# Attention and convolution with fewer VectorE operations, and a chunk mask written into PSUM by VectorE

## The chip, the cores and the metric

The kernel runs on one core of a Trainium2 chip. The metric is the device time of one execution in microseconds. TensorE (PE) multiplies into PSUM; VectorE (DVE) and ScalarE (ACT) read PSUM and SBUF and prepare the next operands; GpSimd (POOL) clears a few buffers, and SyncE (SP) issues the weight loads. Each engine works through its own instructions in the order in which the program lists them, and waits for results of the others through semaphores.

## The reference

Two transformer-like blocks on 512 positions of width 1024, in fp32. The first has 16 meta tokens ahead of the sequence, so 528 positions. The parts that the change touches:

```python
# block 1, differential attention, 8 heads, two maps (m) of width 64 per head, query blocks of 128
s = jnp.einsum('bqhmd,bkhmd->bhmqk', qb * HEAD_DIM ** -0.5, kf)
mask = cid[None, :] <= qc[:, None]                # chunks of 64 positions: no later chunk is seen
p = jax.nn.softmax(jnp.where(mask, s, NEG_INF), axis=-1)
a = p[:, :, 0] - lam * p[:, :, 1]
o = jnp.einsum('bhqk,bkhe->bqhe', a, vf)          # then an RMS norm per head and a gate
# block 1, beside it: a causal depthwise convolution over 31 positions, 1024 channels, with bias
# block 2, third part of its mixer: attention of 4 heads of width 64 over keys chosen by top-k,
#   under the same chunk rule; its first query block sees all admissible keys
```

The convolution's result goes through a layer norm over the channels and a SiLU into the product with `w_conv_out`; that product, gated, is added to the attention's result, and the sum goes into `w_out`. A gated FFN with a short convolution follows. Block 2 has a mixer of three parts (a matrix memory, a linear recurrence and the attention above) and again an FFN.

## The kernel before

The activations lie transposed, channels on the 128 partitions and positions along the free dimension. A weight tile of 1024 x 128 is loaded by SyncE, split by ScalarE (`wh`) and VectorE (`wl`) into two parts, and multiplied in three products per 128 rows (`step`), so that a unit of 128 output channels is 48 products of some 256 columns (`units`, `one`). All products stand on line 314 of the profile, all transposes on line 320, and all VectorE and ScalarE work on line 158, where a wrapper (`Lane`) records it; so rows are told apart by tile names.

The order of the work is made by the Python program itself. It keeps an estimated time for TensorE (`self.pe`), VectorE and ScalarE and an estimated ready time for every tile (`Model`, with 0.13 us from the end of an operation to its use by the next). The main line issues the units; after each group of products `tick` resumes the background tasks, generators that yield the time until their operands are due (`due`). VectorE's background list `bg` is emptied one operation at a time whenever VectorE's estimated time is at most 0.3 us ahead of TensorE's. `until` lets TensorE's estimated time run on until a condition holds. What is fixed so is the order on each engine; on the chip the engines wait for each other where an operand is late.

Block 1's mixer (`block1_mix`) runs 8 convolution units of two weight tiles (`glu`), 32 attention units (q, k, v and gate of 8 heads, `head`) and 8 gate units, in the order of `units1`: one convolution unit, three attention units, and so on, and six gate units at the end. After each convolution unit VectorE forms `u` from PSUM (`e_a`) and the 33 operations of `conv_ops` go into `bg`: a scaling with bias into `a`, a scaling into `b`, 29 taps that alternate between `a` and `b`, `a + b`, and the running sum `csum`. When `bg` is empty after the eighth, `after_conv` starts `layer_norm`: sums over channels, squares, and `finish`, three tasks that produce `us[0]` to `us[7]`. The units of `w_conv_out` (`pairs`) need `us[k]` one after the other; the first two units run together and finish with `us[7]`.

`attention` has two tasks for a head. `softmax(i)` computes the scores of query tile i for both maps (64 rows of the array each) in fp32, adds the mask by a bf16 product of `ind` (ones in one row) with `neg` (-1e30 in 64 columns) for the last 64 keys of the first 64 queries, takes the row maximum, scales it by -0.125 (`nb`) and runs the exponential on ScalarE, with the row sums in `l`. Tile 0 also multiplies the first two queries of the sequence (`sx`). Tiles 0 to 2 hold both maps in one PSUM buffer, tile 3 one map at a time. The second task weighs the two maps (`weigh`), transposes, multiplies by the values, and scales by the norm's factor `sc` in one VectorE operation. Block 2's attention (`sparse`) does the same per head and query tile with three tasks at once; tile 0 is masked by `ind` and `neg`, the others by an identity product with a mask tile. Each step takes a fresh buffer `eT`.

Of the kernel before, what the change touches and what calls it, by code (L numbers as in the profile page):

```python
# [17 lines left out]
P = 128  # L18
# [144 lines left out]
class Build:  # L163
# [159 lines left out]
    def constants(self):  # L323
        nc, c = self.nc, self.const
        self.ident = c.tile([P, P], F32, name="ident")
        make_identity(nc, self.ident)
        self.identb = c.tile([P, P], BF, name="identb")
        nc.vector.tensor_copy(self.identb, self.ident)
        self.ones = c.tile([P, P], F32, name="ones")
        nc.vector.memset(self.ones, 1.0)  # L330
        self.ind = c.tile([P, P], BF, name="ind")
        nc.vector.memset(self.ind, 0.0)
        for m in range(2):
            nc.vector.memset(self.ind[64 * m : 64 * m + 1, 0:64], 1.0)
        self.neg = c.tile([P, 64], BF, name="neg")
        nc.vector.memset(self.neg, NEG)
# [416 lines left out]
    def conv_ops(self, j, u, a, b, csum):  # L753
        V = self.V
        w = lambda k: self.col("conv_dw_w", k * 8 + j)
        ops = [
            lambda: V.tensor_scalar(a, u[:, 0:NQ], w(0), self.col("conv_dw_b", j), op0=MUL, op1=ADD),
            lambda: V.tensor_scalar(b, u[:, 1 : 1 + NQ], w(1), None, op0=MUL),
        ]
        for k in range(2, CK):  # L760
            d = a if k % 2 == 0 else b
            ops.append(lambda k=k, d=d: V.scalar_tensor_tensor(d, u[:, k : k + NQ], w(k), d, op0=MUL, op1=ADD))
        ops.append(lambda: V.tensor_tensor(a, a, b, op=ADD))
        if j == 0:
            ops.append(lambda: V.tensor_copy(csum, a))
        else:
            ops.append(lambda: V.tensor_tensor(csum, csum, a, op=ADD))
        return ops

    def attention(self, tp, h, qk, vs, ctx):  # L770
# [5 lines left out]
        made, used = [], [0]  # L776
        mask = lambda m: (self.ind[64 * m : 64 * m + 64, :], self.neg[64 * m : 64 * m + 64, :])
# [3 lines left out]
        def softmax(i):  # L781
            L = 144 + 128 * i
            q = lambda m: qT[64 * m : 64 * m + 64, 2 + 128 * i : 130 + 128 * i]
            mx, nb, l = self.sm(2, "mx"), self.sm(2, "nb"), self.sm(2, "ll")
            e = self.slot()

            def ex(m, sv):
                S.activation(e[:, m, :L], sv, AF.Exp, bias=nb[:, m : m + 1], scale=0.125, accum_out=l[:, m : m + 1])

            yield self.due(qT)  # L790
            if i < 3:
                i_at, pt = yield from self.at_get()
                for m in range(2):
                    mm(pt[:, 512 * m : 512 * m + L], q(m), k(m, 0, L), True, False)
                for m in range(2):
                    mm(pt[:, 512 * m + L - 64 : 512 * m + L], *mask(m), False, True)
# [12 lines left out]
                self.at_put(i_at)  # L809
            else:  # L810
                for m in range(2):
                    i_at, pt = yield from self.at_get()
                    mm(pt[:, 248:512], q(m), k(m, 0, 264), True, True)
                    mm(pt[:, 512:776], q(m), k(m, 264, 528), True, False)
                    mm(pt[:, 712:776], *mask(m), False, True)
                    yield self.due(pt)
                    V.tensor_reduce(mx[:, m : m + 1], pt[:, 248:776], axis=AX.X, op=MAX)
                    V.tensor_scalar(nb[:, m : m + 1], mx[:, m : m + 1], -0.125, None, op0=MUL)
                    yield self.due(nb)
                    ex(m, pt[:, 248:776])  # L820
                    self.at_put(i_at)
            return e, l
# [7 lines left out]
        def second():  # L830
# [11 lines left out]
            rl0, ss0 = self.sm(4, "rl0"), self.sm(4, "ss0")  # L842
# [46 lines left out]
            v = self.sm(4, "ssv")  # L889
# [6 lines left out]
            o3 = lambda q: o_sb[:, q, :512].rearrange("p (t e) -> p t e", e=P)  # L896
            V.tensor_tensor(o3(1), o3(0), sc[:, :, None].to_broadcast([P, 4, P]), op=MUL)
# [12 lines left out]
    def first_queries(self, ctx, xa, yav):  # L910
# [9 lines left out]
        S.activation(s3, s3, AF.Exp, scale=0.125)  # L920
# [119 lines left out]
    def block1_mix(self, raw):  # L1040
        nc, tc, io, V, S = self.nc, self.tc, self.io, self.V, self.S
        with ExitStack() as es:
# [41 lines left out]
            def glu(s):  # L1084
# [4 lines left out]
                def e_a(p):  # L1089
                    while len(self.bg) > CK + 2:  # L1090
                        self.bg.pop(0)()
# [6 lines left out]
                    self.bg.extend(self.conv_ops(s, u[:, Q0:], cvv(s), hold["tb"][:, 1, :NQ], csum))  # L1098
# [21 lines left out]
            def head(h, i):  # L1120
                def e_q(p):
# [3 lines left out]
                    S.activation(hold["qk"][:, 0, :NQ], p, AF.Copy)  # L1125
# [309 lines left out]
    def block2_mix(self):  # L1435
# [7 lines left out]
        with ExitStack() as es:  # L1443
# [275 lines left out]
            osb, todo = [], list(range(16))  # L1719

            def sparse(n):
# [17 lines left out]
                mx, nb, l, rl = (self.sm(1, x, bufs=5) for x in ("smx", "snb", "sll", "srl"))  # L1739
                V.tensor_reduce(mx, o, axis=AX.X, op=MAX)  # L1740
                V.tensor_scalar(nb, mx, -0.125, None, op0=MUL)
                yield self.due(nb)
                e = tp.tile([P, 3 + SEQ], F32, name=self.nm("e"), tag="lx", bufs=5)
                S.activation(e[:, :L], o, AF.Exp, bias=nb, scale=0.125, accum_out=l)
# [6 lines left out]
                eT = self.flat(SEQ)  # L1751
# [11 lines left out]
            def sparses():  # L1763
                yield from wait("av")
                if not osb:
                    osb.append(self.flat(1024).rearrange("p (t e) -> p t e", e=256))
# [26 lines left out]
            def done(name, o):  # L1793
# [9 lines left out]
                elif kind in ("iq", "mq", "aq", "ak", "lg"):  # L1803
# [6 lines left out]
                    tt(B[kind][-1], o, RB, MUL)  # L1810
# [391 lines left out]
```

## Time and profile before

| | |
|---|---|
| three runs, us | 1582.47, 1582.70, 1582.87 |
| the profiled execution, us | 1582.17 |
| its span, first to last instruction, us | 1580.4 |
| PE, PE weight loads, DVE, ACT, POOL busy, us | 1561.0, 1397.7, 1116.5, 650.8, 26.2 |
| granted TensorE clock, mean | 0.999 |

Busy times are unions of an engine's instructions; a line's "mean ns" is the duration of one instruction, and neighbours overlap, so what an instruction costs its engine is read from its start to the start of the next. In the timeline a merged line "x6" has the time from the first start to the last end. "Idle before" and the views of waits name what ended an engine's idle time. The stages of the span are: loading and first norm to 40 us, block 1's convolution and attention to 367, its layer norm and last attention head to 463, output products and FFN to 700 and on to about 1000, block 2's mixer to 1160, block 2's FFN to the end.

### The profile page before, as it was taken

To read this page: it belongs to the slowest core of one execution; us is meant where nothing else is said; L and a number is where in the kernel's file an instruction comes from. 1 tells how busy PE (TensorE), PEld (TensorE's weight loads), DVE (VectorE), ACT (ScalarE), POOL (GpSimd) and SP (SyncE) were. 2 spreads that over 40 slices of the span, in tenths; PEclk is the share of its full clock that TensorE was granted. 3 is DMA by queue.
4 is the path that set the end of the run, shared out by engine and by line. 5 is a ranking of instruction groups with operands and counts; after the bars stand their busy time and mean duration, and the time that the engine had idled before them with its cause. 6 is when DMAs were issued, how large, how long until landed. Compare 5 with 4: busy or idle time off the path is not lost.

```text
span 1580.4 us, 25476 instructions
## 1 busy us (share of the span) xinstructions
PE 1561.0 (99%) x10349; PEld 1397.7 (88%) x10349; DVE 1116.5 (71%) x2083; ACT 650.8 (41%) x1166; POOL 26.2 (2%) x89
## 2 busy tenths in 40 slices
PE   7999999999999999999999999999999999999998
PEld 6999999999999999999988877797799888888886
DVE  4989999997864676767743357898868877775224
ACT  5344434445542344434432222635466544444122
POOL 3000000000000000000000000000000000000000
PEclk9999999999999999999999999999999999999999
DMA  4322222222222323333333332231054133333221
GB/s 144 95 64 71 68 81 67 68 67 68 67 61 88 103 86 93 94 94 94 89 89 87 91 100 79 67 108 54 5 144 120 54 93 94 93 94 106 95 93 67
DMA packets 233005, 134.17 MB, mean 85 GB/s; under 512 B 6926, under 2 KB 228241, under 8 KB 232889
## 3 DMA queue, kind: packets, MB, share of 16 engines
q1 hardware_dynamic: 231448, 130.35, 28.3%
q8 instruction: 81, 1.33, 0.3%
q0 software_dynamic: 1136, 1.15, 0.3%
q10 hardware_dynamic: 304, 1.05, 0.2%
q14 instruction: 36, 0.29, 0.1%
HBM read 130.44 MB, written 2.10 MB: 84 GB/s over the span
## 4 chain that ended last, share of the span: by engine, by line
PE 98%; ACT 1%; DVE 1%; DMA 0%; issue 0%; DVEq 0%; ACTq 0%; POOLq 0%
PE mm L314 70%; PE at L314 25%; PE at L320 3%; ACT act L158 0%; DMA act<-in_x_dram 0%; DVE yy L158 0%; DVE act L158 0%; ACT ys L158 0%; DVE yc L158 0%; ACT e L158 0%; ACT wh L158 0%; DVE fx L158 0%; DVE res L158 0%; DVEq L2198 0%; ACT rsy L158 0%
## 5 line engine op out<-in xcount | busy, mean ns | idle before, releaser
L314 PE MATMUL mm<-act,wh 128*128 128x256 f32 (+3 forms) x4720 | 907.6, 306 | 1.2 <-ACT act L158 0.5
L314 PEld LDWEIGHTS mm<-act,wh 128*128 128x128 f32 (+1 forms) x4720 | 692.7, 189 | 48.0 <-issue 9.4
L314 PE MATMUL mm<-act,wl 128*128 128x256 f32 (+4 forms) x2360 | 563.1, 303 | 0.0
L158 DVE TENSOR_TENSOR wl<-raw,wh 128x1024 fp32r<-128x1024 f32 (+2 forms) x235 | 284.4, 1211 | 170.4 <-ACT wh L158 168.1
L158 ACT ACTIVATE wh<-raw 128x1024 fp32r<-128x1024 f32 (+2 forms) x235 | 245.7, 1047 | 376.0 <-PE mm L314 195.4
L314 PEld LDWEIGHTS mm<-act,wl 128*128 128x128 f32 (+1 forms) x2360 | 383.2, 189 | 18.1
L158 DVE SCALAR_TENSOR_TENSOR act<-u,par,act 128x514 f32<-128x514 f32 x232 | 160.4, 748 | 0.0
L314 PE MATMUL at<-act,wh 128*128 128x512 f32 x416 | 130.2, 394 | 0.0
L314 PEld LDWEIGHTS at<-act,wh 128*128 128x128 f32 x416 | 78.0, 188 | 18.2
L314 PE MATMUL at<-wh,act 128*128 128x512 f32 x264 | 85.9, 395 | 0.0
L314 PE MATMUL at<-act,act 128*128 128x256 f32 (+8 forms) x468 | 83.8, 328 | 0.0
L314 PE MATMUL mm<-wh,act 128*128 128x256 f32 (+1 forms) x344 | 83.7, 318 | 0.0
L314 PE MATMUL at<-act,wl 128*128 128x512 f32 x208 | 82.1, 394 | 0.0
L158 DVE TENSOR_TENSOR act<-act,act 128x514 f32<-128x514 f32 (+4 forms) x122 | 69.9, 590 | 6.1 <-ACT act L158 5.5
L158 ACT ACTIVATE act<-mm 128x528 f32<-128x528 f32 (+2 forms) x64 | 35.1, 549 | 91.4 <-PE mm L314 91.2
L314 PEld LDWEIGHTS at<-act,act 128*128 128x128 f32 (+1 forms) x468 | 60.7, 189 | 10.1 <-issue 4.0
L158 DVE SCALAR_TENSOR_TENSOR ft<-fx,par,ft 128x512 f32<-128x512 f32 x88 | 65.8, 749 | 1.6
L158 DVE TENSOR_TENSOR fx<-mm,rB 128x514 f32<-128x514 f32 x44 | 30.5, 694 | 50.2 <-PE mm L314 50.0
L158 ACT ACTIVATE act<-at 128x128 f32<-128x128 f32 (+4 forms) x88 | 34.7, 413 | 73.2 <-PE at L314 56.5
L314 PEld LDWEIGHTS mm<-wh,act 128*128 128x128 f32 x344 | 57.8, 189 | 7.1 <-issue 3.2
L158 DVE SCALAR_TENSOR_TENSOR gy<-gx,par,gy 128x512 f32<-128x512 f32 x84 | 62.6, 748 | 1.5
L314 PEld LDWEIGHTS at<-wh,act 128*128 128x128 f32 x264 | 49.6, 188 | 11.4
(290 smaller groups left out, 1463.0 us busy)
## 6 DMA issues: line engine op xcount, KB each, us to landing
raw<-in_w_in_dram SPq DMA_DIRECT2D x82, 512.0 KB, 3.6
raw<-in_w_up_dram SPq DMA_DIRECT2D x44, 512.0 KB, 3.7
raw<-in_ffn_up_dram SPq DMA_DIRECT2D x44, 512.0 KB, 3.9
raw<-in_ffn_down_dram SPq DMA_DIRECT2D x22, 512.0 KB, 3.2
raw<-in_w_out_dram SPq DMA_DIRECT2D x20, 512.0 KB, 3.7
raw<-in_w_down_dram SPq DMA_DIRECT2D x16, 512.0 KB, 3.5
raw<-in_w_conv_out_dram SPq DMA_DIRECT2D x8, 512.0 KB, 3.8
raw<-in_w_down_dram SPq DMA_DIRECT2D x8, 384.0 KB, 3.3
```

The lines of the kernel that those rows point to most:

```text
L158: return f(*a, **k)
L314: self.nc.tensor.matmul(out, lhsT, rhs, start=start, stop=stop)
L320: self.nc.tensor.transpose(out, src, self.ident[p0 : p0 + k, p0 : p0 + k])
```

## The change

VectorE writes the mask: a `memset` of -1e30 into PSUM over the last 64 keys of the first 64 queries, once the scores are there, in both blocks; the bf16 products and their constants go. The queries are multiplied by 0.125 where they leave PSUM, so the exponential needs no scale, and the reduction gives the negated maximum at once. In `weigh` the reciprocals are taken of one column, the first map's sums go to `l0`, whose reciprocal is taken once for a head. The scaling by `sc` becomes four ScalarE operations of 128 columns. The convolution's first tap with the bias becomes a ScalarE operation, issued when `u` is, and the other 30 taps run on one sum; the limit at which `bg` is emptied by force goes from 33 to 31. Block 2's attention shares two `eT` buffers, which are handed on once the products that read them are issued.

```diff
-        self.ind = c.tile([P, P], BF, name="ind")
-        nc.vector.memset(self.ind, 0.0)
-        for m in range(2):
-            nc.vector.memset(self.ind[64 * m : 64 * m + 1, 0:64], 1.0)
-        self.neg = c.tile([P, 64], BF, name="neg")
-        nc.vector.memset(self.neg, NEG)
...
-    def conv_ops(self, j, u, a, b, csum):
+    def conv_ops(self, j, u, a, csum):
         V = self.V
         w = lambda k: self.col("conv_dw_w", k * 8 + j)
-        ops = [
-            lambda: V.tensor_scalar(a, u[:, 0:NQ], w(0), self.col("conv_dw_b", j), op0=MUL, op1=ADD),
-            lambda: V.tensor_scalar(b, u[:, 1 : 1 + NQ], w(1), None, op0=MUL),
-        ]
-        for k in range(2, CK):
-            d = a if k % 2 == 0 else b
-            ops.append(lambda k=k, d=d: V.scalar_tensor_tensor(d, u[:, k : k + NQ], w(k), d, op0=MUL, op1=ADD))
-        ops.append(lambda: V.tensor_tensor(a, a, b, op=ADD))
+        self.S.activation(a, u[:, 0:NQ], AF.Identity, scale=w(0), bias=self.col("conv_dw_b", j))
+        ops = []
+        for k in range(1, CK):
+            ops.append(lambda k=k: V.scalar_tensor_tensor(a, u[:, k : k + NQ], w(k), a, op0=MUL, op1=ADD))
...
-        made, used = [], [0]
-        mask = lambda m: (self.ind[64 * m : 64 * m + 64, :], self.neg[64 * m : 64 * m + 64, :])
+        made, used, l0 = [], [0], self.sm(4, "l0", bufs=4)
...
-                S.activation(e[:, m, :L], sv, AF.Exp, bias=nb[:, m : m + 1], scale=0.125, accum_out=l[:, m : m + 1])
+                S.activation(e[:, m, :L], sv, AF.Exp, bias=nb[:, m : m + 1], accum_out=l if m else l0[:, i : i + 1])
...
-                    mm(pt[:, 512 * m : 512 * m + L], q(m), k(m, 0, L), True, False)
-                for m in range(2):
-                    mm(pt[:, 512 * m + L - 64 : 512 * m + L], *mask(m), False, True)
-                    if i == 0:
+                    mm(pt[:, 512 * m : 512 * m + L], q(m), k(m, 0, L))
+                if i == 0:
+                    for m in range(2):
                         mm(pt[0:2, 512 * m + 256 : 512 * m + 272], qT[64 * m : 64 * m + 64, 0:2], k(m, 0, 16))
                 yield self.due(pt)
+                V.memset(pair(pt)[0:64, :, L - 64 : L], NEG)
...
-                V.tensor_reduce(mx, pair(pt)[:, :, :L], axis=AX.X, op=MAX)
-                V.tensor_scalar(nb, mx, -0.125, None, op0=MUL)
+                V.tensor_reduce(nb, pair(pt)[:, :, :L], axis=AX.X, op=MAX, negate=True)
...
-                    mm(pt[:, 512:776], q(m), k(m, 264, 528), True, False)
-                    mm(pt[:, 712:776], *mask(m), False, True)
+                    mm(pt[:, 512:776], q(m), k(m, 264, 528), True, True)
                     yield self.due(pt)
-                    V.tensor_reduce(mx[:, m : m + 1], pt[:, 248:776], axis=AX.X, op=MAX)
-                    V.tensor_scalar(nb[:, m : m + 1], mx[:, m : m + 1], -0.125, None, op0=MUL)
+                    V.memset(pt[0:64, 712:776], NEG)
+                    V.tensor_reduce(nb[:, m : m + 1], pt[:, 248:776], axis=AX.X, op=MAX, negate=True)
...
-                rl, kap = self.sm(2, "rl"), self.sm(1, "kap")
+                rl, kap = self.sm(1, "rl"), self.sm(1, "kap")
                 V.reciprocal(rl, l)
-                V.scalar_tensor_tensor(kap, l[:, 0:1], rl[:, 1:2], self.nlam, op0=MUL, op1=MUL)
-                V.tensor_copy(rl0[:, i : i + 1], rl[:, 0:1])
+                V.scalar_tensor_tensor(kap, l0[:, i : i + 1], rl, self.nlam, op0=MUL, op1=MUL)
...
-            v = self.sm(4, "ssv")
+            v, rl0 = self.sm(4, "ssv"), self.sm(4, "rl0")
+            V.reciprocal(rl0, l0)
...
-            o3 = lambda q: o_sb[:, q, :512].rearrange("p (t e) -> p t e", e=P)
-            V.tensor_tensor(o3(1), o3(0), sc[:, :, None].to_broadcast([P, 4, P]), op=MUL)
+            yield self.due(sc)
+            for i in range(4):
+                b = slice(i * P, (i + 1) * P)
+                S.activation(o_sb[:, 1, b], o_sb[:, 0, b], AF.Copy, scale=sc[:, i : i + 1])
...
-                    while len(self.bg) > CK + 2:
+                    while len(self.bg) > CK:
...
-                    S.activation(hold["qk"][:, 0, :NQ], p, AF.Copy)
+                    S.activation(hold["qk"][:, 0, :NQ], p, AF.Copy, scale=0.125)
...
-                mm(o, B["aq"][hp][r64, t * P : t * P + P], B["ak"][hp][r64, :L], True, False)
-                if t == 0:
-                    mm(o[:, L - 64 :], self.ind[r64, :], self.neg[r64, :], False, True)
-                else:
+                mm(o, B["aq"][hp][r64, t * P : t * P + P], B["ak"][hp][r64, :L], True, t == 0)
+                if t:
                     mm(o, self.identb, self.mbs[:, 512 * (t - 1) : 512 * (t - 1) + L], False, True)
                 yield self.due(pt)
...
+                if t == 0:
+                    V.memset(o[0:64, L - 64 :], NEG)
+                nb, l, rl = (self.sm(1, x, bufs=5) for x in ("snb", "sll", "srl"))
+                V.tensor_reduce(nb, o, axis=AX.X, op=MAX, negate=True)
...
-                eT = self.flat(SEQ)
+                while not ets:
+                    yield 0.1
+                eT = ets.pop()
...
+                ets.append(eT)
...
-                    tt(B[kind][-1], o, RB, MUL)
+                    if kind == "aq":
+                        stt(B[kind][-1], o, 0.125, RB, MUL, MUL)
+                    else:
+                        tt(B[kind][-1], o, RB, MUL)
```

## Rows read from the trace of the kernel before

**Rows 1.** The profile's page: busy time and instructions of each engine, and the chain that ended last, by engine.

```profile
PE 1561.0 (99%) x10349; PEld 1397.7 (88%) x10349; DVE 1116.5 (71%) x2083; ACT 650.8 (41%) x1166; POOL 26.2 (2%) x89
...
PE 98%; ACT 1%; DVE 1%; DMA 0%; issue 0%; DVEq 0%; ACTq 0%; POOLq 0%
```

**Rows 2.** What TensorE waited for over the whole span, longest total first: us in total, times, longest.

```profile
PE mm L320 <- DMA act<-in_x_dram: 4.9, 3, 2.7
PE at L320 <- DVE act L158: 2.7, 1, 2.7
...
PE at L320 <- ACT e L158: 1.1, 1, 1.1
```

**Rows 3.** Busy time of each engine by stage: the stretch, its length, then PE, PE weight loads, DVE, ACT and POOL busy us with their instructions, the granted clock, the DMA share and GB/s.

```profile
116.00:367.00 251.00, 251.00 (x2027) 237.30 (x2026) 232.73 (x478) 104.66 (x269) 0.50 (x4) 1.00 0.24 71
367.00:463.00 96.00, 96.00 (x775) 89.97 (x773) 69.53 (x170) 51.37 (x118) 3.86 (x11) 1.00 0.23 64
1085.00:1160.00 75.00, 73.19 (x483) 57.90 (x481) 58.62 (x162) 36.54 (x95) 0.20 (x2) 1.00 0.10 29
```

**Rows 4.** Groups of TensorE's products by shape over the whole span: the mask products, and the small products for the first two queries.

```profile
L314 PE MATMUL at<-neg,ind 64*128 64x64 bf16 x68 | 9.7, 190 | 0.0
...
L314 PE MATMUL at<-act 64*2 64x16 f32 x32 | 3.2, 173 | 0.0
```

**Rows 5.** TensorE's timeline around the masks of head 0, query tiles 0, 1 and 3: start, duration, operation, merged count.

```profile
78.07 0.19 PE L314 MATMUL at<-neg,ind 64*128 64x64 bf16 x1
78.19 0.20 PE L314 MATMUL at<-act 64*2 64x16 f32 x2
78.32 0.20 PE L314 MATMUL at<-neg,ind 64*128 64x64 bf16 x1
78.45 0.20 PE L314 MATMUL at<-act 64*2 64x16 f32 x2
78.58 0.33 PE L320 MATMUL at<-ident,act 128*128 128x128 f32 x1
...
83.45 0.20 PE L314 MATMUL at<-neg,ind 64*128 64x64 bf16 x2
83.57 0.39 PE L314 MATMUL mm<-act,wh 128*128 128x256 f32 x1
...
96.98 0.19 PE L314 MATMUL at<-neg,ind 64*128 64x64 bf16 x1
97.09 0.39 PE L314 MATMUL mm<-act,wh 128*128 128x264 f32 x1
```

**Rows 6.** VectorE's timeline in four places: taps of the first channel tile, a softmax and a weighing of head 0, the end of the second channel tile (last tap, a + b and csum), and two taps of the FFN's convolution.

```profile
61.65 4.07 DVE L158 SCALAR_TENSOR_TENSOR act<-u,par,act 128x514 f32<-128x514 f32 x6
...
80.62 0.43 DVE L158 TENSOR_REDUCE mx<-at 128x2 f32<-128x288 f32 x1
81.09 0.17 DVE L158 TENSOR_SCALAR nb<-mx 128x2 f32<-128x2 f32 x1
81.17 0.21 DVE L158 COPY act<-vt 16x128 f32<-16x128 f32 x1
...
82.50 0.15 DVE L158 COPY rl<-rl 128x1 f32<-128x1 f32 x1
...
107.34 1.43 DVE L158 TENSOR_TENSOR act<-act,act 128x514 f32<-128x514 f32 x2
...
602.86 1.54 DVE L158 SCALAR_TENSOR_TENSOR ft<-fx,par,ft 128x512 f32<-128x512 f32 x2
```

**Rows 7.** Groups of VectorE's operations by shape over the whole span: busy us, mean ns of one, idle us before. The convolution's scalings, the scaling of the attention's output, an operation on 64 columns of PSUM, and a memset of 64 partitions by 64 columns in SBUF.

```profile
L158 DVE TENSOR_SCALAR act<-u,par 128x514 f32<-128x514 f32 x16 | 7.8, 515 | 0.2
...
L158 DVE TENSOR_TENSOR act<-act,sc 128x512 f32<-128x512 f32 x8 | 5.5, 691 | 0.3
...
L158 DVE TENSOR_SCALAR act<-at,srl 128x64 f32<-128x64 f32 x16 | 4.2, 277 | 3.2 <-PE at L314 3.1
...
L158 DVE MEMSET sc<- 64x64 f32 x3 | 0.3, 112 | 0.2
```

**Rows 8.** Groups of ScalarE's operations by shape over the whole span: a tap of the FFN's convolution with scale and bias columns on 512 columns, and an operation on 128 columns with a column operand.

```profile
L158 ACT ACTIVATE ft<-fx,par 128x512 f32<-128x512 f32 x44 | 35.5, 809 | 0.1
...
L158 ACT ACTIVATE act<-act,aa 128x128 f32<-128x128 f32 x20 | 7.3, 391 | 2.1 <-DVE act L158 1.1 <-PE at L314 1.0
```

**Rows 9.** VectorE's operations on the tile u alone (u itself, the two scalings and the taps), by stretch: length, then DVE busy us and count, POOL busy, clock, DMA. First three intervals from one u to the next, then from the last u to the convolution's end, then the whole stage.

```profile
110.40:149.10 38.70, 20.26 (x30) 0.00 (x0) 1.00 0.24 69
149.10:185.50 36.40, 18.33 (x27) 0.12 (x1) 1.00 0.25 74
185.50:220.60 35.10, 18.18 (x27) 0.12 (x1) 1.00 0.26 75
...
298.10:367.00 68.90, 30.73 (x46) 0.00 (x0) 1.00 0.22 65
...
116.00:367.00 251.00, 129.13 (x191) 0.50 (x4) 1.00 0.24 71
```

**Rows 10.** VectorE's timeline at the layer norm: its first operation after the convolution's end, the last subtraction that makes us[7], and the first operation on the result of the first pair of w_conv_out units, with the idle time before it.

```profile
367.05 0.43 DVE L158 TENSOR_SCALAR act<-act 128x514 f32<-128x514 f32 x1
...
454.59 0.69 DVE L158 TENSOR_TENSOR act<-act,act 128x514 fp32r<-128x514 f32 x1 [0.88 <-ACT act L158]
...
462.47 0.69 DVE L158 SCALAR_TENSOR_TENSOR act<-act,mm 128x514 f32<-128x514 f32 x1 [5.98 <-PE mm L314]
```

More of the change, by code (lines that the diff above doesn't have):

```diff
@@ L783, in softmax @@
             q = lambda m: qT[64 * m : 64 * m + 64, 2 + 128 * i : 130 + 128 * i]
-            mx, nb, l = self.sm(2, "mx"), self.sm(2, "nb"), self.sm(2, "ll")
+            nb, l = self.sm(2, "nb"), self.sm(1, "ll")
             e = self.slot()
             def ex(m, sv):
-                S.activation(e[:, m, :L], sv, AF.Exp, bias=nb[:, m : m + 1], scale=0.125, accum_out=l[:, m : m + 1])
+                S.activation(e[:, m, :L], sv, AF.Exp, bias=nb[:, m : m + 1], accum_out=l if m else l0[:, i : i + 1])
             yield self.due(qT)
@@ L841, in second @@
             o_sb = self.slot()
-            rl0, ss0 = self.sm(4, "rl0"), self.sm(4, "ss0")
+            ss0 = self.sm(4, "ss0")
             def weigh(i, e, l):
                 L = 144 + 128 * i
-                rl, kap = self.sm(2, "rl"), self.sm(1, "kap")
+                rl, kap = self.sm(1, "rl"), self.sm(1, "kap")
                 V.reciprocal(rl, l)
-                V.scalar_tensor_tensor(kap, l[:, 0:1], rl[:, 1:2], self.nlam, op0=MUL, op1=MUL)
-                V.tensor_copy(rl0[:, i : i + 1], rl[:, 0:1])
+                V.scalar_tensor_tensor(kap, l0[:, i : i + 1], rl, self.nlam, op0=MUL, op1=MUL)
                 V.scalar_tensor_tensor(e[:, 0, :L], e[:, 1, :L], kap, e[:, 0, :L], op0=MUL, op1=ADD)
@@ L919, in first_queries @@
         yield self.due(s3)
-        S.activation(s3, s3, AF.Exp, scale=0.125)
+        S.activation(s3, s3, AF.Exp)
         yield self.due(s3)
@@ L1097, in e_a @@
                     self.until(lambda: "params" in state)
-                    self.bg.extend(self.conv_ops(s, u[:, Q0:], cvv(s), hold["tb"][:, 1, :NQ], csum))
+                    self.bg.extend(self.conv_ops(s, u[:, Q0:], cvv(s), csum))
                 if s == 0:
@@ L1718, in block2_mix @@
             STEPS = [(t, h) for t in range(4) for h in range(4)]
-            osb, todo = [], list(range(16))
+            osb, todo, ets = [], list(range(16)), []
             def sparse(n):
@@ L1732, in sparse @@
                 o = pt[:, :L]
-                mm(o, B["aq"][hp][r64, t * P : t * P + P], B["ak"][hp][r64, :L], True, False)
-                if t == 0:
-                    mm(o[:, L - 64 :], self.ind[r64, :], self.neg[r64, :], False, True)
-                else:
+                mm(o, B["aq"][hp][r64, t * P : t * P + P], B["ak"][hp][r64, :L], True, t == 0)
+                if t:
                     mm(o, self.identb, self.mbs[:, 512 * (t - 1) : 512 * (t - 1) + L], False, True)
                 yield self.due(pt)
-                mx, nb, l, rl = (self.sm(1, x, bufs=5) for x in ("smx", "snb", "sll", "srl"))
-                V.tensor_reduce(mx, o, axis=AX.X, op=MAX)
-                V.tensor_scalar(nb, mx, -0.125, None, op0=MUL)
+                if t == 0:
+                    V.memset(o[0:64, L - 64 :], NEG)
+                nb, l, rl = (self.sm(1, x, bufs=5) for x in ("snb", "sll", "srl"))
+                V.tensor_reduce(nb, o, axis=AX.X, op=MAX, negate=True)
                 yield self.due(nb)
                 e = tp.tile([P, 3 + SEQ], F32, name=self.nm("e"), tag="lx", bufs=5)
-                S.activation(e[:, :L], o, AF.Exp, bias=nb, scale=0.125, accum_out=l)
+                S.activation(e[:, :L], o, AF.Exp, bias=nb, accum_out=l)
                 self.at_put(i)
@@ L1765, in sparses @@
                 if not osb:
+                    ets.extend(halves(self.slot()))
                     osb.append(self.flat(1024).rearrange("p (t e) -> p t e", e=256))
```

## The prediction

> **What bounds the kernel now.** I read the page's busy table first. TensorE is busy for 1561.0 of 1580.4 us, VectorE for 71% of the span and ScalarE for 41%, and the chain that ended last is 98% TensorE [rows 1]. The list of what TensorE waited for comes next. Its longest entry is the input at the start, and for results of VectorE and ScalarE it waits a few us in all [rows 2]. So this kernel costs the sum of its products. An edit can gain in two ways only, by taking products away or by removing one of the few waits, and it can lose in one way, by making TensorE wait. The table by stage says where that is near. From 116 to 367 us (convolution and attention) TensorE has no idle time and VectorE is busy for 232.7 of 251 us; from 367 to 463 us (layer norm) it is 69.5 of 96; from 1085 to 1160 us (second attention) TensorE itself has 1.8 us idle [rows 3].
>
> The profiled execution took 1582.2 us, 1.8 us more than its span; the median of the runs is 1582.7. My sum is a difference and I take it from the median.
>
> **The products taken away.** 68 mask products go: two for each of three query tiles and two for the fourth, in 8 heads, and 4 in the second block [rows 4]. I price each from its start to the start of what follows, since their own 190 ns overlap with neighbours. In head 0 these are 0.12 and 0.13 us in tile 0, 0.12 us for both of tile 1 together (different halves of the array, side by side), and 0.11 us for one of tile 3 [rows 5]. Tile 2 is taken like tile 1. A head then gives 0.12 + 0.13 + 0.12 + 0.12 + 2 x 0.11 = 0.71 us, eight heads 5.7 us, the second block's two pairs 0.25 us: **6.0 us**. In tile 0 the small products for the first two queries stand apart, 0.13 us each, because a mask lies between them [rows 4, 5]. After the change they are neighbours on different halves, and may run side by side as the masks of tile 1 do: 0 to 1.0 us, I take 0.5. Nothing replaces these products on TensorE. Together **-6.5 us**.
>
> The Trainium skill prices a product otherwise ("VectorE: DVE Perf Modes", The TRN2 errata): at least 60 cycles, or 6 plus the columns, which would be an estimated 29 ns for 64 columns and 2.0 us in all. The rows show about four times that.
>
> **The convolution.** Before, a channel tile is two scalings, 29 taps, the addition of the two partial sums and the addition into the running sum. Taps alternate between two partial sums, so neighbours are independent: six taps in 4.07 us, hence (4.07 - 0.75)/5 = 0.66 us from start to start. Two taps in a row on one sum, as the FFN has them, take 1.54 us, hence 0.79 [rows 6]. A tap that needs its neighbour's result costs 0.12 us more. After, all 30 taps run on one sum. Gone are two scalings (0.515 us each [rows 7], 0.08 of it overlapped, as 0.75 against 0.66 for a tap: 0.86) and one addition (0.73, half of the pair at 107.34 [rows 6]); new are one tap (0.66) and 0.12 us for each tap that directly follows a tap. Other operations stand between some of them and hide it. The bounds are no follower, -0.93 us a channel, and all 29, +2.6. I take 20, since the timeline shows runs of taps broken by weight splits and softmax steps: **+1.5 us a channel**. The first tap moves to ScalarE: 8 times 0.81 us [rows 8], in a queue that is free for 146 of 251 us [rows 3]. It waits there for VectorE's u; behind it stand weight splits and evictions of PSUM, which TensorE needs a unit later (48 products of 0.12 us, 5.8 us), so a wait of one or two VectorE operations is covered. No DMA moves, and GpSimd's memset of u stays ahead.
>
> The Trainium skill says the opposite of chains (same page, The DRAIN you can't avoid, and its rules: reduce the number of operations, the semaphore costs nothing extra). By it the channel costs -0.93 us, and the first rival's time follows. The rows, 0.79 against 0.66, contradict it here.
>
> **Attention on VectorE.** A softmax loses the scaling of the maximum: the reduction no longer has a dependent neighbour (0.12) and the operation itself goes (81.09 to 81.17, 0.08): 0.20 us, five times a head [rows 6]. It gains a memset into PSUM, which no row shows. The nearest are a memset of 64x64 in SBUF (0.11 us) and an operation on 64 columns of PSUM with a column operand (0.28) [rows 7]. I take the first, the same kind and shape, 0.18 for the three of 2x64, plus 0.12 as the reduction now depends on it: 3 x 0.30 + 2 x 0.23 = 1.4 us, by the upper row 2.0. The scaling of the output goes to ScalarE (0.69 off VectorE [rows 7]; there four operations near 0.39 us [rows 8]), one small reciprocal comes (0.2). The copies of rl cost nothing now: they start and end while the next operation waits for kap [rows 6]. Sum -1.0 + 1.4 - 0.69 + 0.2 = **-0.1 us a head** (-0.4 to +0.5). The memset waits for TensorE where the reduction did, with the same work queued behind. The start-up memsets end long before the input arrives; the scale inside an eviction or a multiply costs at most 0.06 us in places with slack.
>
> **Where VectorE's extra time shows.** Convolution work fills whatever VectorE has left. A channel is 32 operations in the view by tile, u among them; in three of the intervals between two u's VectorE does 30, 27 and 27, and 46 are left from the last u on [rows 9]. So it is behind, and its end (367 us) follows its cost. From 116 to 367 us it holds 129 of 251 us (with u, without the additions) [rows 9]; the rest is paced by TensorE. Six channels at +1.4 us are 8.4 us, and divided by 129/251 the end comes 16 us later. If instead the 18 us that VectorE idles there [rows 3] can be filled, it is 0. I take **10 us**, between the two.
>
> Behind it hangs the layer norm, 367.05 to 455.3 us, whose last result the first pair of w_conv_out units needs. That pair ends at 462.47 [rows 10], its last 12 products of 0.12 us start at 461.0: a margin of 5.7 us. TensorE will come 5.5 us earlier, so the margin is gone and every us of lateness is a wait, less what is given back: the layer norm has 26 us of VectorE idle time around it [rows 3], much of it waiting for TensorE-paced neighbours, which fall away once TensorE waits itself, and TensorE can do head 7's products meanwhile. I take 7 of the 10 us as given back, **+3 us**. This is my weakest number.
>
> **The second attention.** Sixteen scalings fall out of chains (0.2 us each, three chains). Two shared buffers instead of a fresh one each add a wait when three tasks meet, with the task's PSUM buffer held meanwhile. TensorE idles 1.8 us there [rows 3]: -1 to +2 us, taken as 0.
>
> **Sum:** 1582.7 - 6.5 + 3.0 = **1579.2 us**.
>
> **The rivals.**
> - *No wait at the layer norm.* VectorE fills its idle time, or dependent taps are mostly separated. For it: 18 us idle; against: the growing backlog [rows 9]. 1582.7 - 6.5 = 1576.2.
> - *Slower: the layer norm is late in full.* The convolution ends 16 us late and only 3 us come back: +13 - 6.5, 1589. It decides from a wait of 6.5 us on. For it: TensorE's margin is used up by its own gain; against: the layer norm's many waits.
> - *The products gain little*: half of their time is the array's change from one kind of product to the next and falls on the next product, 3.2 us instead of 6.5, with 1 us of wait, 1580.5. Against it: a score product is followed by its mask and the mask by the next product, so there is a change either way [rows 5]. The skill's 60-cycle figure would put it near here.
> - *The shared buffers delay the second attention* by 3 us on top of the forecast: 1582.2.
>
> **How the numbers follow.** My forecast (a wait of 1 to 6 us) has 0.38, no wait 0.29, slower 0.19, little gain 0.05, second attention 0.09. The measurement separates 0.2%, 3.2 us. The forecast's centre lies at -3.5, so a little over half of it counts as faster: 0.21 + 0.29 = 0.50; same 0.17 + 0.14 = 0.31; slower 0.19. The range runs from the full pairing without any wait and a shorter second attention, 1575, to the late layer norm, 1588.
>
> **What would show it.** Right: 64 plus 4 mask products gone and TensorE's busy time 6 to 7 us lower; taps 0.78 us apart in runs; the convolution's end near 372 to 377 us of the new trace; a wait of TensorE for VectorE results between 440 and 465 us, a few us long; VectorE's busy time there up. Wrong: no wait there (first rival), a wait over 6 us (second), waits at transposes or scores in 116 to 367 us, meaning that a memset or ScalarE's new work is late, or more idle time between 1085 and 1160 us.

## The result and the profile after

The changed kernel takes 1598.55 us (median of 4, 1597.81 to 1599.57) against 1582.59: 16 us slower, ratio 1.0097, interval 1.0085 to 1.011. The profiled execution took 1599.57 us, the longest of the four; its span is 1597.8.

Busy time of each engine (page), then the chain that ended last:

```profile
PE 1569.2 (98%) x10279; PEld 1401.1 (88%) x10281; DVE 1116.9 (70%) x2019; ACT 668.7 (42%) x1206; POOL 26.6 (2%) x89
...
PE 94%; DVE 3%; DMA 1%; ACT 1%; issue 1%; DVEq 0%; ACTq 0%; POOLq 0%
```

Against [rows 1] TensorE has 70 products fewer in the records (68 masks; some records are missing) and yet 8 us more busy time, and VectorE stands on the chain with 3%. VectorE executes 64 operations fewer and is busy for as long as before: an operation taken away is not time taken away.

The stages of [rows 3]:

```profile
116.00:367.00 251.00, 251.00 (x2001) 236.40 (x2000) 222.17 (x428) 116.18 (x298) 0.62 (x5) 1.00 0.25 72
367.00:463.00 96.00, 88.99 (x675) 80.55 (x674) 81.05 (x191) 50.61 (x121) 3.06 (x11) 0.94 0.22 61
...
1085.00:1160.00 75.00, 74.40 (x430) 55.50 (x429) 62.65 (x162) 38.45 (x101) 0.10 (x1) 1.00 0.10 29
```

In the first, VectorE is busy for 10 us less than before although it has a backlog. In the second, TensorE has 7 us idle, a granted clock of 0.94, and 100 products fewer behind it. What it waited for, over the whole span (some of the entries):

```profile
PE mm L314 <- ACT act L158: 4.8, 3, 3.1
...
PE at L320 <- ACT act L158: 1.9, 1, 1.9
PE mm L314 <- DVE act L158: 1.8, 4, 1.0
```

In the first entry ScalarE is only the last link: it splits what VectorE has just made of us[k]. The second, 1.9 us, is another wait and comes with the change. The transposes of head 7's output wait for the scaling by `sc`, which VectorE had until now; on ScalarE it stands behind the split of a weight tile (ScalarE's timeline, then TensorE's, whose next products wait for us[0] in any case):

```profile
449.96 1.05 ACT L158 ACTIVATE wh<-raw 128x1024 fp32r<-128x1024 f32 x1
450.91 1.27 ACT L158 ACTIVATE act<-act,sc 128x128 f32<-128x128 f32 x4
...
451.35 1.22 PE L320 MATMUL at<-ident,act 128*128 128x128 f32 x4 [1.92 <-ACT act L158]
455.69 0.80 PE L314 MATMUL mm<-act,wh 128*128 128x256 f32 x2 [3.12 <-ACT act L158]
```

VectorE's timeline shows the cause of the others. First six taps in a row, then the first operation of the layer norm, the last two subtractions that make us, and the first eviction of w_conv_out's first pair:

```profile
386.63 4.70 DVE L158 SCALAR_TENSOR_TENSOR act<-u,par,act 128x514 f32<-128x514 f32 x6
...
409.40 0.41 DVE L158 TENSOR_SCALAR act<-act 128x514 f32<-128x514 f32 x1
...
469.46 1.30 DVE L158 TENSOR_TENSOR act<-act,act 128x514 fp32r<-128x514 f32 x2
477.95 0.69 DVE L158 SCALAR_TENSOR_TENSOR act<-act,mm 128x514 f32<-128x514 f32 x1 [7.19 <-PE mm L314]
```

Taps are (4.70 - 0.75)/5 = 0.79 us apart, against 0.66 [rows 6]. The layer norm starts 42.4 us later than in [rows 10], ends at 470.8 instead of 455.3, and the pair's eviction is 15.5 us late, most of the 17.4 us by which the span is longer (1597.8 against 1580.4). TensorE in that time, and its clock (length, busy us and count, granted clock, DMA):

```profile
448.00:452.00 4.00, 2.08 (x13) 1.00 0.18 54
452.00:456.00 4.00, 0.88 (x3) 0.55 0.07 19
456.00:460.00 4.00, 2.91 (x11) 0.50 0.39 112
...
468.00:472.00 4.00, 3.82 (x15) 0.50 0.00 2
472.00:476.00 4.00, 4.00 (x32) 0.89 0.01 4
```

It runs out of products at 449.4. The clock falls from 2.4 to 1.2 GHz at 452.4, after 1.9 us of idle time and in the four transposes shown above, and TensorE works at 1.2 GHz until 472.9. The backlog is in VectorE's operations on the tile u (DVE busy and count, then ACT, POOL), from the fifth u to the sixth and from the last u to the convolution's end:

```profile
185.10:220.30 35.20, 18.60 (x26) 0.82 (x1) 0.12 (x1) 1.00 0.26 74
...
301.00:408.00 107.00, 45.76 (x61) 0.82 (x1) 0.00 (x0) 1.00 0.24 70
```

26 operations between two u's where 31 arrive (u and 30 taps); 61 are left after the last u, against 46 in [rows 9].

### The profile page after: what moved, and what is told of

Its sections match the earlier page's. It is cut to its first block, busy times and chain, and to the rows that moved or that the text cites. A ratio compares the mean times of both kernels' runs of the same rounds, so it can differ in the third digit from the quotient of the medians.

```text
span 1597.8 us, 25321 instructions
## 1 busy us (share of the span) xinstructions
PE 1569.2 (98%) x10279; PEld 1401.1 (88%) x10281; DVE 1116.9 (70%) x2019; ACT 668.7 (42%) x1206; POOL 26.6 (2%) x89
## 4 chain that ended last, share of the span: by engine, by line
PE 94%; DVE 3%; DMA 1%; ACT 1%; issue 1%; DVEq 0%; ACTq 0%; POOLq 0%
PE mm L314 68%; PE at L314 24%; PE at L320 3%; DVE act L158 2%; ACT act L158 1%; DMA raw<-in_w_out_dram 1%; DMA act<-in_x_dram 0%; DVE wl L158 0%; DMA raw<-in_ffn_up_dram 0%; DVE yy L158 0%; ACT wh L158 0%; DVE rsa L158 0%; DVE rsy L158 0%; ACT ys L158 0%; DVE yc L158 0%
## 5 line engine op out<-in xcount | busy, mean ns | idle before, releaser
L314 PEld LDWEIGHTS mm<-act,wh 128*128 128x128 f32 (+1 forms) x4720 | 696.2, 190 | 60.1 <-issue 11.9
L158 DVE SCALAR_TENSOR_TENSOR act<-u,par,act 128x514 f32<-128x514 f32 x240 | 180.4, 752 | 6.1 <-ACT act L158 0.9
L314 PE MATMUL at<-act,act 128*128 128x256 f32 (+9 forms) x468 | 83.6, 329 | 0.8 <-ACT act L158 0.7
L158 DVE TENSOR_TENSOR act<-act,act 128x514 f32<-128x514 f32 (+4 forms) x114 | 64.4, 583 | 2.6 <-ACT act L158 2.1
L314 PEld LDWEIGHTS mm<-wh,act 128*128 128x128 f32 x344 | 57.9, 188 | 7.3 <-issue 3.4
L158 ACT ACTIVATE act<-at 128x128 f32<-128x128 f32 (+6 forms) x88 | 34.4, 412 | 67.9 <-PE at L314 50.5
```

Source lines behind the costliest of these rows:

```text
L158: return f(*a, **k)
L314: self.nc.tensor.matmul(out, lhsT, rhs, start=start, stop=stop)
```

## The experiments

Theory 1: the chain of dependent taps delays the convolution, and TensorE waits at the layer norm. Theory 2, the rival: the memsets and new waits of the attention delay VectorE. The table has the time (median, beside before's 1582.6 to 1583.1 of the same chips), the ratio with its interval, and from the trace the start of the layer norm, the end of the last us, the first eviction of the pair, and TensorE's idle time between 430 and 480 us.

| kernel | us | ratio | layer norm | last us | pair | idle |
|---|---|---|---|---|---|---|
| before | 1582.6 | | 367.0 | 455.3 | 462.5 | 0.1 |
| after | 1598.6 | 1.0097 [1.0085, 1.011] | 409.4 | 470.8 | 478.0 | 8.2 |
| e_alt: after, two sums | 1577.9 | 0.9964 [0.995, 0.9978] | 356.9 | 437.3 | 459.7 | 0.1 |
| e_chain: before, one sum | 1595.5 | 1.0074 [1.006, 1.0088] | 403.7 | 470.1 | 477.1 | 6.6 |
| e_mask: before, memsets | 1591.5 | 1.0051 [1.0037, 1.0065] | 387.7 | 463.6 | 470.8 | 6.6 |
| e_nomask: before, no masks | 1579.6 | 0.9981 [0.9968, 0.9995] | 365.1 | 450.0 | 461.2 | 2.0 |
| e_att: after, old convolution | 1584.1 | 1.0007 [0.9998, 1.0015] | 365.9 | 450.5 | 463.3 | 3.2 |
| e_first4 | 1585.7 | 1.0015 [1.0006, 1.0024] | 383.9 | 461.7 | 467.5 | 4.1 |
| e_last4 | 1590.7 | 1.0046 [1.0032, 1.006] | 380.6 | 461.9 | 469.6 | 5.2 |
| e_inter | 1593.1 | 1.0061 [1.0048, 1.0074] | 408.6 | 470.0 | 471.6 | 7.5 |
| e_fill | 1598.4 | 1.0098 [1.0083, 1.0112] | 409.2 | 470.6 | 476.6 | 4.9 |
| e_taps_act | 1584.1 | 1.0009 [0.9996, 1.0022] | 363.1 | 446.4 | 463.8 | 0.1 |

**e_alt**, the changed kernel with two sums:

```diff
         self.S.activation(a, u[:, 0:NQ], AF.Identity, scale=w(0), bias=self.col("conv_dw_b", j))
+        self.S.activation(b, u[:, 1 : 1 + NQ], AF.Copy, scale=w(1))
         ops = []
-        for k in range(1, CK):
-            ops.append(lambda k=k: V.scalar_tensor_tensor(a, u[:, k : k + NQ], w(k), a, op0=MUL, op1=ADD))
+        for k in range(2, CK):
+            d = a if k % 2 == 0 else b
+            ops.append(lambda k=k, d=d: V.scalar_tensor_tensor(d, u[:, k : k + NQ], w(k), d, op0=MUL, op1=ADD))
+        ops.append(lambda: V.tensor_tensor(a, a, b, op=ADD))
```

> The changed kernel with one thing different: the taps run on two partial sums again, in turn. Both first taps are ScalarE operations, 29 taps and the addition of the two sums stay on VectorE, so VectorE has as many operations as in the changed kernel (one ScalarE operation more for each channel tile); only the dependence of neighbours goes. Theory 1 (the chain of dependent taps delays the layer norm): taps in a row 0.66 to 0.67 us apart, the convolution ends before 375 us, TensorE has under 2 us of idle time between 440 and 480 us, 1577 to 1582 us. Theory 2 (the memsets and the attention's new waits delay VectorE): the convolution's end stays near 408 us, 1594 to 1599 us.

1577.9: with as many VectorE operations and all memsets, 20.6 us faster than the change and faster than both kernels. The layer norm starts 52 us earlier, TensorE doesn't idle at it. Theory 1 holds for the change as it stands, and ScalarE's new work can't be the cause, since there is one operation more of it for each channel. Some 2 of the 20.6 us lie elsewhere, in the FFN (under after_again).

**e_chain**, the kernel before with only the new convolution (first tap on ScalarE and limit 31 too, as in the change):

```diff
...
-            ops.append(lambda k=k, d=d: V.scalar_tensor_tensor(d, u[:, k : k + NQ], w(k), d, op0=MUL, op1=ADD))
+            ops.append(lambda k=k: V.scalar_tensor_tensor(a, u[:, k : k + NQ], w(k), a, op0=MUL, op1=ADD))
```

> The kernel before with the convolution of the changed kernel alone: first tap on ScalarE, 30 taps on one sum, limit 31. Masks, scales and attention as before. Theory 1: the convolution ends near 395 to 410 us, TensorE idles and falls to the lower clock between 445 and 475 us, 1595 to 1601 us. Theory 2: 1580 to 1585 us.

1595.5, as theory 1 has it: the convolution alone costs 12.5 us. With the 1.4 of e_att, the rest of the change, that makes 13.9 of the 16.

**e_mask** and **e_nomask**, the kernel before with the mask alone changed, and with the mask left out (there without the last line):

```diff
-                    mm(pt[:, 512 * m + L - 64 : 512 * m + L], *mask(m), False, True)
...
                 yield self.due(pt)
+                V.memset(pair(pt)[0:64, :, L - 64 : L], NEG)
```

> The kernel before with the mask alone changed: the 68 mask products and their constants go, VectorE writes -1e30 into PSUM before each row maximum; maximum, scale, convolution and the rest as before. If the whole time from each mask product to the next product is saved, as the prediction has it, 6.5 us less: 1576 us. If part of it falls on the score product ahead of it, as the changed kernel's trace suggests (score products 0.22 us before, 0.31 us after, where a full product follows), 3 to 4 us less: 1579 us. Theory 2 (the memset delays VectorE so that TensorE waits): 1584 us or more.

> The kernel before without the 68 mask products and without anything in their place, so the chunk mask is left out of the first block and of the first query tile of the second. It prices the products alone. Saved in full: 1576 us. Saved in part: 1579 us. The difference from the run with memsets is what the memsets cost: 0 to 0.5 us if VectorE has room for them, more if not.

The products alone give 3.4 us in the median (the single executions scatter, 1577.2 to 1586.0), not 6.5. That is no clean price: without them TensorE idles for 2.0 us at the layer norm, its clock is 1.2 GHz from 463.1 to 466.5 us, and its busy time is 4.6 us less than before (1556.4 us). The price is worked out from slots below. The memsets alone cost 11.9 us more: theory 2 isn't false, it is the same mechanism with another cause. VectorE has little room left in this stage, and what the memsets add arrives at the layer norm, 22.6 us later than in e_nomask.

**e_att**, the changed kernel with the old convolution (two scalings, two sums, limit 33):

```diff
...
-        self.S.activation(a, u[:, 0:NQ], AF.Identity, scale=w(0), bias=self.col("conv_dw_b", j))
+            lambda: V.tensor_scalar(a, u[:, 0:NQ], w(0), self.col("conv_dw_b", j), op0=MUL, op1=ADD),
+            lambda: V.tensor_scalar(b, u[:, 1 : 1 + NQ], w(1), None, op0=MUL),
```

> The changed kernel with the convolution of the kernel before put back whole (two scalings, 29 taps in turn on two sums, addition, limit 33): what is left is the change of mask, attention and second block. Theory 1 (only the dependent taps bring the delay): VectorE's attention work is no more than before (slots of before and after: 0.82 and 0.81 us for a maximum with all that belongs to it, 0.94 and 0.96 for a weighing, 0.4 less for the output scaling), so the convolution ends within 5 us of 367 and the time is 1577 to 1581 us. Theory 2 (the memsets bring a good part, as the run with the mask alone suggests): the end lies beyond 375 us, 1585 us or more.

The layer norm starts at 365.9, as before: what the attention lost pays for the memsets. But the time is 1584.1, between the two expectations, since TensorE meets two new waits. One of 2.0 us is at the first pair of w_conv_out. TensorE's timeline, then VectorE's:

```profile
461.60 0.40 PE L314 MATMUL mm<-act,wl 128*128 128x256 f32 x2
464.01 0.74 PE L314 MATMUL mm<-act,wh 128*128 128x256 f32 x4 [2.02 <-DVE act L158]
```

```profile
460.62 0.16 DVE L158 TENSOR_TENSOR ssv<-ssv,ss 128x4 f32<-128x4 f32 x1 [6.93 <-ACT act L158]
...
463.20 0.16 DVE L158 TENSOR_TENSOR sc<-rsy,rl 128x4 f32<-128x4 f32 x1
463.28 0.68 DVE L158 SCALAR_TENSOR_TENSOR act<-act,mm 128x514 f32<-128x514 f32 x1
```

The eviction that frees TensorE's buffer stands behind the 14 small operations of head 7's norm, 0.2 us each. In the kernel before they came after it. The other wait, 1.2 us at 434, is for ScalarE's eviction of aT. Against e_alt, which has the two scalings on ScalarE, this kernel is 6.2 us slower.

**e_first4** and **e_last4**: e_alt with the chain in half of the channel tiles (e_last4 with `j >= 4`; the other branch is e_alt's).

```diff
+        if j < 4:
+            for k in range(1, CK):
+                ops.append(lambda k=k: V.scalar_tensor_tensor(a, u[:, k : k + NQ], w(k), a, op0=MUL, op1=ADD))
+        else:
...
```

> The kernel with two partial sums again (e_alt), but with the chain on one sum in channel tiles 0 to 3. Half the dependent taps, 6 us of VectorE time. If every channel's cost is carried along as a backlog and ends up, divided by the convolution's share of VectorE (0.47), in the end of the convolution, it ends 13 to 20 us later than in e_alt (365 to 372 us) and TensorE waits 0 to 3 us: 1578 to 1581 us. If the first channels' cost is absorbed because there was no backlog yet, as the prediction assumed for two of them, the end lies under 362 us and the time is that of e_alt.

> As the run before it, with the chain in channel tiles 4 to 7 instead. Backlog theory: the same end of the convolution as with tiles 0 to 3, within 5 us, 1578 to 1581 us. If only the late channels count: 10 us or more later than with tiles 0 to 3, and 3 us or more slower.

The convolution ends 27 and 24 us later than in e_alt, so it doesn't matter which channels pay: early cost is carried along as backlog, not absorbed. Both ends are later than I had worked out, and so are the times: 7.8 and 12.7 us over e_alt. The second is 5 us worse though its layer norm starts no later: its pair comes 2.1 us later, and 2.7 us lie in the FFN products between 550 and 820 us (under after_again).

**e_inter**, the changed kernel with the first pair's two units in turn for each us[k]:

```diff
...
+            for q, k in enumerate(order[: kt - 1]):
+                self.until(lambda: have(k))
+                for u, outs in enumerate(outs_list):
+                    self.step(outs, ws[u], acts[k], k, q == 0, False)
```

> The changed kernel with the first two units of w_conv_out taken in turn for each us[k], instead of the second after the first; the rest as it is. If the wait consists of VectorE's lateness alone, the time stays at 1598. If part of it is TensorE's own order (42 products of the second unit stand behind the first, which waits for us[k] one by one), these 5 us move into the waits: 1592 to 1595 us.

1593.1, 5.5 us less with VectorE as late as before (last us 470.0). So a third of the loss was TensorE's own order: 42 products of the second unit stood behind a first unit that waited for us[k] one by one. The clock is also back at 2.4 GHz earlier, at 459.8 us; e_fill has the clock alone.

**e_fill**, the changed kernel with filler products in that wait:

```diff
+                n = 0
+                while fill is not None and u == 0 and not have(k):
+                    self.pe += 0.1
+                    self.tick()
+                    n += 1
+                    if n % 3 == 2 and not have(k):
+                        self.nc.tensor.matmul(fill, self.ident, self.ones, start=True, stop=True)
```

> The changed kernel with filler products (the identity times a matrix of ones, fp32, 128 columns) into unused columns of the second unit's PSUM buffer while the first unit of w_conv_out waits for us[k], at about two thirds of the planned wait. They compute nothing that is used. They keep TensorE busy, so that its clock stays up, and change nothing on VectorE. If VectorE alone sets the time of the wait: no change, 1597 to 1599 us. If the lower clock costs much behind the wait: 1592 to 1596 us. From the rows of the changed kernel (full clock again at 472.6 us, the last us at 470.8) I expect 1 to 2 us: 1597 us.

The same stretches as above, with the fillers:

```profile
448.00:452.00 4.00, 4.00 (x32) 1.00 0.05 16
452.00:456.00 4.00, 4.00 (x37) 1.00 0.11 32
456.00:460.00 4.00, 2.34 (x16) 1.00 0.33 99
...
468.00:472.00 4.00, 3.86 (x30) 1.00 0.01 2
472.00:476.00 4.00, 4.00 (x35) 1.00 0.00 0
```

The clock stays at 2.4 GHz, the pair ends 1.4 us earlier, and the time is the same within its interval. The lower clock looked worth about 7 us (some 14 us of busy time at it), but the products that it slowed would have waited for VectorE anyway: TensorE still idles for 4.9 us there.

**e_taps_act**, the kernel before with both scalings on ScalarE:

```diff
-            lambda: V.tensor_scalar(a, u[:, 0:NQ], w(0), self.col("conv_dw_b", j), op0=MUL, op1=ADD),
-            lambda: V.tensor_scalar(b, u[:, 1 : 1 + NQ], w(1), None, op0=MUL),
+        self.S.activation(a, u[:, 0:NQ], AF.Identity, scale=w(0), bias=self.col("conv_dw_b", j))
+        self.S.activation(b, u[:, 1 : 1 + NQ], AF.Copy, scale=w(1))
```

> The kernel before with the two scalings of the convolution moved to ScalarE (29 taps in turn on two sums and the addition stay on VectorE); mask and attention as before. VectorE loses about 0.9 us a channel tile. If TensorE sets the time and VectorE had no wait to give, the convolution ends 10 us or more earlier and the time stays within 1.5 us of before: 1581 to 1584 us. If the gain of e_alt came from VectorE being relieved and not from the products: 1578 us.

Seven of its twelve executions lie between 1582.1 and 1585.0 us, five between 1587.4 and 1589.4 (below); without those it is before's time. Where TensorE doesn't wait, room on VectorE is worth nothing by itself. It is what lets e_alt take the memsets: e_att, without that room, is 6.2 us slower.

**after_again**, for a second profile:

> The changed kernel once more, for a second profile. In the first, the 2100 products of the FFN between 550 and 820 us took 2.2 us longer than before, about 1 ns each. If that belongs to the change it stands in this profile too; if it varies from execution to execution it is another size here.

1599.1. Against the kernel before, products between 550 and 820 us lose 2.4 us here too, as in the first profile. e_mask, e_last4, e_inter and e_fill show it, e_alt, e_chain and e_first4 don't; no part of the change goes with it, and the cause stays open. So some 2 of the 16 us are not the layer norm's.

## Why the prediction was wrong

**The products, -6.5 us: mis-sized, -3.4.** The rival that gave 3.2 us and 0.05 of the chance had the right size. I priced a mask from its start to the next start, 0.12 us [rows 5]. The rows after the change show what that left out, scores of a fourth tile and what follows them:

```profile
95.07 1.16 PE L314 MATMUL at<-act 64*128 64x264 f32 x4
96.16 0.52 PE L314 MATMUL mm<-act,wh 128*128 128x264 f32 x2
```

The last of these four scores starts at 95.85, and the next full product 0.31 us later. With a mask between them [rows 5] it was 0.34 (last score at 96.75, mask 96.98, full product 97.09): nearly all of the mask's slot passes without it too, between the score and the full product. Over all heads the masks' 6.18 us go, the last scores become 3.77 us longer, and the small products for the first two queries get 1.0 shorter: 3.4 us net, and 2.4 of it the masks'. (The further busy time that e_nomask saves lies in weight products, whose slots differ by as much among these kernels.) My argument against this rival, that there is a change of kind either way, assumed that the change costs the same after a mask as after a score. The Trainium skill's figure ("VectorE: DVE Perf Modes", The TRN2 errata), an estimated 2.0 us for all 68, was nearer to the net 2.4 than my 6.0. Per mask that is an estimated 29 ns against 35 net (2.41 us over 68). The intervals that I took from the trace are right, 91 ns in the mean (6.18 us over 68), three times the estimate and not four as I wrote, but an interval is not a price.

**The convolution's own cost, +1.5 us a channel: right.** Counted from each tap's start to the next operation (idle gaps over 0.1 us left out), 30 taps now take 0.761 us each, 22.8 us a channel, where 31 operations of 0.665 and an addition of 0.69 took 21.3: +1.53, or 12.2 us for all eight. The Trainium skill's rule (same page, The DRAIN you can't avoid), by which the channel would cost 0.93 us less, does not hold here. e_alt shows it with equal counts: 0.686 for the same slot, 2.25 us less a channel with its addition counted, and 20.6 us less kernel time in all.

**The convolution's end, 10 us later: the step that failed.** The layer norm starts 42 us later. First, I counted six channels and left the early ones out; e_first4 and e_last4 show that all eight count, 12.2 us. Second, I let VectorE's 18 idle us take up part of it. From the first u to the last tap VectorE's idle time grew instead, from 25.1 us to 40.4 (in 327 and 359 us); 5 of these are the short gaps behind dependent taps, which the 12.2 hold already. What grew are the waits for scores (5.0 us to 9.9, up to the layer norm) and for ScalarE's part of a weight split (5.3 to 9.1). Third, the division by 129/251 makes only 24 us of 12.2. The rest of the 42 is other work of VectorE that now stands ahead of the layer norm: some 10 us among the taps, and 9 us behind the last tap, where the last addition into csum comes after a head's softmax and weighing:

```profile
395.76 3.12 DVE L158 SCALAR_TENSOR_TENSOR act<-u,par,act 128x514 f32<-128x514 f32 x4
...
403.60 0.37 DVE L158 SCALAR_TENSOR_TENSOR act<-act,kap 128x144 f32<-128x144 f32 x1
...
406.97 0.68 DVE L158 TENSOR_TENSOR act<-act,act 128x514 f32<-128x514 f32 x1
```

A us of VectorE cost moved the start of the layer norm by 2.6 to 3.1 us in these kernels: 11.9 us (by its own trace) by 36.6 in e_chain; against e_alt, 9.0 us by 27.0 in e_first4 and by 23.7 in e_last4, and 18.0 by 52.5 in the change. Why the idle time grows with the load is not settled.

**What is given back, 7 of 10 us: the share was luck.** The layer norm took 61.4 us instead of 88.2, so 27 of the 42 came back, 0.63 against my 0.7. I expected it from idle time, and that gives 10 (VectorE idles for 20.4 us in the layer norm before, for 10.8 after). The other 17 are work. VectorE is busy there for 67.8 us before and for 50.6 after, with 5 weight splits instead of 11 and 3 row maxima instead of 8; up to the last us both kernels do the same 59 splits and 40 row maxima. So that part of the 42 was no lateness, but work that moved ahead of the layer norm.

**The wait at the layer norm, 3 us.** It is where the prediction put it, between 440 and 465 us, but longer: TensorE idles for 8.2 us and works at 1.2 GHz for some 14 more. The last us comes 15.5 us late and so does the pair, so that the margin of 5.7 us took nothing off: e_inter takes 5.5 us off without touching VectorE. I had measured the margin at the last us only; with all eight late, each us[k] holds up the first unit, and the second unit's products can't fill the gaps. In kernel time a us of VectorE cost 0.9 to 1.4 us: 12.5 us for 11.9 in e_chain, 20.6 for 18.0 against e_alt, 7.8 and 12.7 for 9.0 in e_first4 and e_last4. My sum had 3 us of time for 8.4 of VectorE.

**The attention, -0.1 us a head: right, and not harmless.** A memset of 64x64 in PSUM takes 0.112 us, as in SBUF [rows 7], one of 2x64 0.165, which was my choice of bounds. e_att's layer norm starts within 1.1 us of before. But the moved work changed the order on VectorE and ScalarE, and 3.2 us of new waits in e_att ate the products' gain.

**The second attention, 0, and the shared buffers: no delay.** TensorE's longest wait there fell from 1.1 us [rows 2] to 0.6, and from the first row sum's reciprocal to the last the attention takes 57.2 us instead of 57.9, in e_alt and e_att too. That rival is refuted; the sign is the other way.

So the slower rival (0.19) was the case, beyond its 1589. It had 13 us of lateness at the last us, where 15.5 came, took 6.5 us for the products, where 3.4 came, and nothing for the 2 us in the FFN. The range ended at 1588, short even of that rival's time.

## What to carry to other kernels

Where a second engine is 90% busy beside the bounding one and feeds a later stage in order, price an edit on it in full, a us of its cost as about a us of kernel time here, and not against the idle time that a table shows. Fewer operations are no gain if they become a chain: the taps on two sums (e_alt) beat both kernels, 1577.9 us. And the price of an instruction is the difference between what stands around it with it and without it, not its own slot.

## What the runs showed of the hardware

**The clock falls in some executions of a kernel and not in others.** The kernel before and e_taps_act have a TensorE wait of 1.1 us in the second attention. In the profiled execution of e_taps_act, one of its five long ones, the clock falls behind it (5 us each: busy and count, clock); in that of the kernel before it stays at 2.4 GHz:

```profile
1140.00:1145.00 5.00, 3.78 (x23) 1.00 0.00 0
1145.00:1150.00 5.00, 5.00 (x20) 0.54 0.62 183
1150.00:1155.00 5.00, 4.67 (x18) 0.50 0.09 27
1155.00:1160.00 5.00, 4.88 (x41) 0.94 0.00 0
```

It costs some 5 us, and the mean clock of the five is 0.995, that of most others 0.999. The kernel before has executions of that time and mean clock too (7 of 55 in the three rounds of runs), though none of them has a trace. e_alt and e_att, with waits of 0.6 us there, have none in 16; that is too few to show a gain of the change.

**The clock fell without idle time too.** In e_alt it is 1.2 GHz from 439.6 to 443.0 us, though TensorE is busy throughout from 432 to 444; just before it fell, from 436.2 to 439.1, it ran four scores on 64 rows and 16 products on 16 rows.

**A small 64-row product between a 64-row product and a full one is nearly free.** Followed by another score a score's slot is 0.22 us, followed by a full product 0.31; the mask between them added 0.03, and 0.035 in the mean of all 68.

**A dependent tap costs 0.12 us more.** A tap that follows another tap starts 0.665 us after it on two sums and 0.787 us after it on one.
